# Attention sink as a 129th score column, the u product by halves of positions, and an even table of fillers

## The chip, the cores and the metric

The kernel runs on one core of a Trainium2 chip. The metric is the device time of one execution in microseconds (us), the median of several; smaller is better. The core has five engines with instruction queues of their own: TensorE (PE; its weight loads are counted apart as PEld), VectorE (DVE), ScalarE (ACT), GpSimd (POOL) and SyncE (SP), which here issues DMA transfers. Engines wait for each other through semaphores.

## The reference

One layer of a hybrid decoder trunk on 1024 positions of width 1024, in float32. Only the first third matters here:

```
h = rmsnorm(x)
[q | k | v | u | s | gate_a | gate_b] = h @ w_in
A: q, k by heads of 64, RMS norm; windowed attention in blocks of 128 queries against
   the 256 keys of the block before and of its own; scores minus slope * distance;
   softmax over these and one learned "sink" per head, whose weight is then dropped
B: u * (tril(W_s) @ rmsnorm(v) + b), in chunks of 128 positions
x = x + (sigmoid(gate_a) * (A @ w_oa) + sigmoid(gate_b) * (B @ w_ob)) @ w_out
x = x + down(silu(conv(up_g)) * conv(up_v))
```

There are 8 query heads, 2 key heads, and 8 blocks of 128 queries. The products want more than one pass at the fast matmul type, so an operand is split into a high part (`...h`) and a low part (`...l`, the operand minus the high part), and three products hh, hl and lh are summed (`mm3`).

## The kernel before, in words

The program starts with the products for k, v and the first q, then runs the attention loop, then the V phase (rmsnorm of v, the triangular products), the gates, the output product, and for most of the time the feed-forward part. The change lies in the attention loop and in two constants that it uses.

The loop has 20 steps. A unit of attention work, n = 0 to 15, is four heads of one block of queries (half n // 8, block n % 8), and it goes down a pipeline of several steps. All engines take their instructions in the order in which the loop is written. Step n issues on TensorE: the scores of unit n (`s_mm`, tile `sc`, eight matmuls of 128x256), the products with v of unit n-4 (`pv_mm`, tile `pv`), a first filler, the transposes of the probabilities of unit n-2 (`p_trans`, tile `pt`), a second filler, and the transposes of q for unit n+2 (`q_trans`, tile `pqt`). The two fillers are what the table FILL says for that step, one letter each: q is a q projection (`q_proj`, 24 matmuls of 128x256), u is one sixteenth of the u product (`u_chunk`, 12 matmuls of 128x512), v is half of the v product for one block of positions (`v_half`, 24 matmuls of 128x256, tile `pvs`).

What the other engines do for a unit, in the order of its steps:

- `s_mask`: VectorE picks the masked scores (copy_predicated; each query sees a window of 128 of the 256 keys, so the two halves of the keys fold into one tile of 128x4x128), and adds the distance penalty `ali`, which gives `c`.
- `s_max`: VectorE takes the row maximum, then the negated maximum against the negated sink (`nsink`), then the sink less the maximum. These go into the small tile `sm`.
- `s_exp`, one step later: ScalarE takes four exponentials (one for each head, with the row sum) and a small one of the sink, VectorE adds that to the sums and takes the reciprocal, GpSimd multiplies `c` by it.
- `p_split`: ScalarE copies the transposed tile to `ch`, VectorE makes `cl`, and GpSimd separates each into the keys of the block before (`eh`, `el`) and of the own block (`ch`, `cl`) by four affine_selects.
- `pv_out`: ScalarE and VectorE add the two halves of `pv` into `ya`, which SyncE stores after the last block of a half.

A u chunk covers two of the eight blocks of the contraction and all 1024 positions: four chunks make one tile `pu` of two PSUM banks, which VectorE then evacuates into uT in one instruction of 128x1024 (L679). `pu` and `sc` come from the same pool (`PS`, two buffers of two banks each) and take turns. `pt`, `pv`, `pq`, `pqt` and two of the `pvs` tiles come from another (`PH`, one bank each).

GpSimd's queue holds more than this: the low parts of weights that arrive during the loop (`weights(n)`: ScalarE makes the high part, GpSimd the low part; v0 at step 13, v1 at 14, z0 at 16, z1 at 17), and, towards the end, the triangular mask of s (L792) and its low part (L795). The load of s (L99) uses a raw buffer that v1's split sets free. After unit 15, input rows are loaded again (`rows_again(1)`, L617) into the buffer of `ya`.

Of the kernel before, what the change touches and what calls it, by code (L numbers as in the profile page):

```python
# [10 lines left out]
F = mybir.dt.float32  # L11
R = mybir.dt.float32r
U8 = mybir.dt.uint8
AF = mybir.ActivationFunctionType
# [9 lines left out]
NEG = -1e30  # L24
# [3 lines left out]

ROWS = (slice(0, 64), slice(64, 128))
X_AHEAD = 5  # L30
FILL = "qu|q|qu|qu|uu|q|qu|qu|q|qu|qu|qu|q|uu|u|u|uu|vv|v|v".split("|")
WHEN = {"u1": 0, "q0": 1, "q1": 2, "u2": 5, "u3": 9, "v0": 13, "v1": 14, "z0": 16, "z1": 17}


# [7 lines left out]
def body(ctx, tc, nc, a):  # L42
# [8 lines left out]
    def nm(s):  # L51
        uid[0] += 1
        return f"{s}_{uid[0]}"
# [37 lines left out]
    def mm3(out, wh, wl, mh, ml, first, last, **kw):  # L91

        nc.tensor.matmul(out, wh, mh, start=first, stop=False, **kw)  # L93
        nc.tensor.matmul(out, wh, ml, start=False, stop=False, **kw)  # L94
        nc.tensor.matmul(out, wl, mh, start=False, stop=last, **kw)  # L95
# [231 lines left out]
    nc.vector.tensor_scalar(kgq, cp[:, 184:185], cp[:, 185:186], 0.125, op0=ALU.mult, op1=ALU.mult)  # L327
# [118 lines left out]
    def s_mask(n):  # L446

        half, b = divmod(n, 8)
        p4 = st.pop(("ps", n))
        hs = slice(4 * half, 4 * half + 4)  # L450
        c = tm.tile([128, 4, 128], F, tag="c", name=nm("c"), bufs=3)
        if b == 0:
            nc.vector.tensor_tensor(c, p4[:, :, 0:128], ali[:, hs, :], op=ALU.add)
            nc.gpsimd.affine_select(out=c, in_=c, pattern=[[0, 4], [-1, 128]], compare_op=ALU.is_ge,
                                    fill=NEG, base=0, channel_multiplier=1)
        else:
            nc.vector.copy_predicated(p4[:, :, 128:256], msk, p4[:, :, 0:128])
            nc.vector.tensor_tensor(c, p4[:, :, 128:256], ali[:, hs, :], op=ALU.add)
        st[("c0", n)] = c

    def s_max(n):
        hs = slice(4 * (n // 8), 4 * (n // 8) + 4)
        c = st.pop(("c0", n))
        sm = tm.tile([128, 4, 4], F, tag="sm", name=nm("sm"), bufs=3)
        nc.vector.tensor_reduce(sm[:, 0, :], c, axis=AX.X, op=ALU.max)
        nc.vector.scalar_tensor_tensor(sm[:, 0, :], sm[:, 0, :], -1.0, nsink[:, hs], op0=ALU.mult, op1=ALU.min)
        nc.vector.tensor_tensor(sm[:, 2, :], sink_b[:, hs], sm[:, 0, :], op=ALU.add)
        st[("c", n)] = (c, sm)

    last_exp, last_sel = [None], [None]  # L470

    def s_exp(n):
        c, sm = st[("c", n)]
        m, den, es = sm[:, 0, :], sm[:, 1, :], sm[:, 2, :]
# [3 lines left out]
        nc.scalar.activation(es, es, AF.Exp)  # L478
        nc.vector.tensor_tensor(den, den, es, op=ALU.add)
        nc.vector.reciprocal(den, den)  # L480
        nc.gpsimd.tensor_tensor(c, c, den.unsqueeze(2).to_broadcast([128, 4, 128]), op=ALU.mult)

    def p_trans(n):
        c = st.pop(("c", n))[0]
        p = PH("pt")
        for i in range(4):
            nc.tensor.transpose(p[:, i * 128:(i + 1) * 128], c[:, i, :], ident)
        st[("pt", n)] = p.rearrange("p (h q) -> p h q", q=128)
# [58 lines left out]

    n_q, n_u, n_v, u_done = [4], [0], [0], []
    pvs = {}
# [9 lines left out]
    def filler(n, i):  # L559

        kind = FILL[n][i:i + 1]
        if kind == "q":
            q_proj(n_q[0])
            n_q[0] += 1
            return [n_q[0] - 1]
        if kind == "v":
            v_half(n_v[0], 0)
            n_v[0] += 1
        if kind == "u":
            t = u_chunk(n_u[0])  # L570
            n_u[0] += 1
            if t is not None:
                u_done.append((t, ust["p"]))
        return []

    wv = []
# [70 lines left out]
    for n in range(20):  # L647
# [27 lines left out]
            x_sums((0, 1), True)  # L675
        if n == 19:
            x_sums((2, 3), True)
        for t, p in u_done:
            nc.vector.tensor_tensor(uT[:, t, :], p, rstd_b, op=ALU.mult)  # L679
        u_done.clear()  # L680
        if n + 2 < 16:
            q_trans(n + 2)
# [1295 lines left out]
def layout(x, mix_norm, w_in, q_norm, k_norm, sinks, sgu_norm, w_s, b_s,  # L1978
# [35 lines left out]
    ali = -slopes[None, :, None] * dist[:, None, :]  # L2014
# [31 lines left out]
```

## Time and profile before

| | us |
| --- | --- |
| median of 3 runs (range) | 1183.58 (1183.52 to 1184.87) |
| span of the profiled execution | 1183.5 |
| TensorE busy in the span | 1170.3 |
| VectorE busy | 874.5 |
| GpSimd busy | 631.8 |
| ScalarE busy | 566.5 |
| attention loop from step 2 to its end | 59 to 180 |

A line of the profile gives the engine, the line of the kernel, the operation, output and input by their names in the program, and the shape. In a timeline the first two numbers are the start and the duration in us; a wait stands in brackets with what ended it. Groups have their count, busy time and mean in ns. The profiled execution's own time is its span but for what lies ahead of the first instruction and behind the last, and at 1183.5 it is at the median of the runs.

### The profile page before, as it was taken

What the parts mean: (1) busy time and instruction counts of PE and PEld (TensorE: products, weight loads), DVE (VectorE), ACT (ScalarE), POOL (GpSimd) and SP (SyncE); (2) the same over time, 40 slices, a digit from 0 to 9 for tenths busy, and PEclk for the clock granted to TensorE, in tenths of its full rate; (3) what the DMA queues carried; (4) which work ended last, traced back from release to release, by engine and by line L of the source; (5) the groups of instructions that cost most, each with busy time, mean ns of one, the idle gap of its engine ahead of it and who ended that gap; (6) DMA issues with size and microseconds to landing.
All of it is one profiled execution on the core that took longest, in us unless ns stands there. A gap on an engine that the chain in (4) does not pass through costs nothing.

```text
span 1183.5 us, 15928 instructions
## 1 busy us (share of the span) xinstructions
PE 1170.3 (99%) x5842; PEld 990.4 (84%) x5842; DVE 874.5 (74%) x1037; ACT 566.5 (48%) x878; POOL 631.8 (53%) x435
## 2 busy tenths in 40 slices
PE   8999999999999999999999999999999999999998
PEld 8989989988888878888878888888888888888887
DVE  7798975743536776678788788877888797875674
ACT  8555667644336653335444443444444445425331
POOL 2467685488884764444867677776767541000000
PEclk9999999999999999999999999999999999999999
DMA  7110136157556654454545445455555268975471
GB/s 272 37 55 19 54 130 228 56 168 239 161 160 204 233 193 154 146 176 132 138 129 169 118 149 152 142 141 134 166 137 160 72 219 287 365 232 196 155 231 67
DMA packets 80942, 188.66 MB, mean 159 GB/s; under 512 B 9184, under 2 KB 16864, under 8 KB 80736
## 3 DMA queue, kind: packets, MB, share of 16 engines
q1 hardware_dynamic: 73008, 167.58, 40.7%
q0 software_dynamic: 7456, 15.73, 8.0%
q10 hardware_dynamic: 400, 4.33, 1.1%
q8 instruction: 46, 0.75, 0.3%
q14 instruction: 32, 0.26, 0.1%
HBM read 146.97 MB, written 49.02 MB: 166 GB/s over the span
## 4 chain that ended last, share of the span: by engine, by line
PE 82%; DVE 4%; POOL 3%; ACT 2%; issue 2%; DMA 1%; DVEq 0%; POOLq 0%; SPq 0%; ACTq 0%
PE pz L1060 50%; PE pd L1855 10%; PE pdy L1855 8%; PE px L95 2%; PE px L93 2%; PE px L94 2%; PE pu L95 1%; PE pu L93 1%; PE pu L94 1%; PE pv L517 1%; PE pq L93 1%; PE pq L95 1%; PE pq L94 1%; DVE xa L621 1%; DMA lq<-wup 0%
## 5 line engine op out<-in xcount | busy, mean ns | idle before, releaser
L1060 PE MATMUL pz<-T,qh 128*128 128x512 f32 x472 | 145.6, 390 | 0.0
L1060 PE MATMUL pz<-B,ph 128*128 128x512 f32 x352 | 109.7, 393 | 0.7 <-ACT x L1695 0.7
L1060 PEld LDWEIGHTS pz<-T,qh 128*128 128x128 f32 x472 | 88.4, 188 | 18.6 <-ACT u L885 0.3
L1019 POOL TENSOR_TENSOR pl<-lp,ph 128x1024 fp32r<-128x1024 f32 x30 | 73.2, 2439 | 52.9 <-ACT ph L89 52.9
L1060 PE MATMUL pz<-T,ql 128*128 128x512 f32 x236 | 91.8, 389 | 0.0
L1019 POOL TENSOR_TENSOR ql<-lq,qh 128x1024 fp32r<-128x1024 f32 x30 | 76.8, 2559 | 9.1 <-ACT qh L89 9.1
L1060 PEld LDWEIGHTS pz<-B,ph 128*128 128x128 f32 x352 | 65.1, 188 | 16.7 <-ACT x L1695 3.8
L1078 DVE TENSOR_TENSOR pz<-pz,rstd_b 128x1024 f32<-128x1024 f32 x60 | 73.9, 1232 | 4.6 <-ACT rstd_b L143 2.5
L1060 PE MATMUL pz<-T,s3h 128*128 128x512 f32 x232 | 71.4, 389 | 0.0
L1060 PE MATMUL pz<-y,wjh 128*128 128x512 f32 x224 | 69.5, 391 | 0.6 <-POOL y L1233 0.3
L1060 PE MATMUL pz<-B,pl 128*128 128x512 f32 x176 | 68.6, 390 | 0.0
L1855 PE MATMUL pd<-bh,ah 128*128 128x512 f32 x176 | 68.5, 389 | 0.0
L1855 PE MATMUL pd<-bl,ah 128*128 128x512 f32 x176 | 68.5, 389 | 0.0
L1855 PE MATMUL pd<-bh,al 128*128 128x512 f32 x176 | 68.5, 389 | 0.0
L1060 PE MATMUL pz<-T,AX 128*128 128x512 f32 x264 | 63.4, 389 | 0.0
L1060 PE MATMUL pz<-B,AX 128*128 128x512 f32 x264 | 63.4, 389 | 0.0
L1019 POOL TENSOR_TENSOR s3l<-lq,s3h 128x512 fp32r<-128x512 f32 x20 | 26.0, 1298 | 62.3 <-ACT s3h L89 62.3
L1060 PEld LDWEIGHTS pz<-T,AX 128*128 128x128 f32 x264 | 49.5, 188 | 10.3
L1060 PEld LDWEIGHTS pz<-B,AX 128*128 128x128 f32 x264 | 49.6, 188 | 10.3
L89 ACT ACTIVATE AX<-lr 128x1024 fp32r<-128x1024 f32 x22 | 23.4, 1063 | 70.9 <-POOL lr L621 70.9
L621 DVE TENSOR_TENSOR pz<-pz,u 128x512 f32<-128x512 f32 x37 | 25.9, 700 | 42.5 <-ACT u L1072 36.2
L1550 DVE SCALAR_TENSOR_TENSOR tg<-pz,cp,tg 128x1023 f32<-128x1023 f32 (+1 forms) x44 | 56.2, 1278 | 0.8
(359 smaller groups left out, 3597.6 us busy)
## 6 DMA issues: line engine op xcount, KB each, us to landing
lp<-wup SPq DMA_DIRECT2D x22, 512.0 KB, 3.8
lq<-wup SPq DMA_DIRECT2D x22, 512.0 KB, 4.2
ra<-wdown SPq DMA_DIRECT2D x44, 256.0 KB, 4.9
b<-T SPq DMA_DIRECT2D x44, 256.0 KB, 3.5
lq<-wup POOLq DMA_DIRECT2D x42, 256.0 KB, 5.3
B<-tv SPq DMA_DIRECT2D x33, 256.0 KB, 2.0
T<-tt SPq DMA_DIRECT2D x33, 256.0 KB, 2.1
b<-B SPq DMA_DIRECT2D x33, 256.0 KB, 3.0
```

What stands on the lines that cost most here:

```text
L89: return nc.scalar.activation(dst, src, AF.Copy, scale=scale)
L93: nc.tensor.matmul(out, wh, mh, start=first, stop=False, **kw)
L94: nc.tensor.matmul(out, wh, ml, start=False, stop=False, **kw)
L95: nc.tensor.matmul(out, wl, mh, start=False, stop=last, **kw)
L517: nc.tensor.matmul(o, vhl[:, kb, g, :], w[:, 2 * g:2 * g + 2, :], start=i == 0 and g == 0, stop=i == len(ops) - 1, skip_group_check=True)
L621: eng.tensor_tensor(out, x, y, op=op)
L1019: nc.gpsimd.tensor_tensor(l, r, h.bitcast(F), op=ALU.subtract)
L1060: nc.tensor.matmul(o, p[:, k, :], m, start=not more and k == 0 and j == 0, stop=k == nk - 1 and j == 2, skip_group_check=True)
L1078: nc.vector.tensor_tensor(z, z, rstd_b, op=ALU.mult)
L1550: nc.vector.scalar_tensor_tensor(t[:, j:], p[:, 0:1024 - j], cw[:, ci, 2 - j:3 - j], t[:, j:], op0=ALU.mult, op1=ALU.add)
L1855: nc.tensor.matmul(o[d], p[:, k - k0, m], q[:, k - k0, :], start=new and k == 0 and j == 0, stop=k == HK - 1 and j == 2, skip_group_check= ...
```

## The change

Three edits in the attention loop.

The sink becomes a column of the tile. The tile is now 129 wide for each head: 128 columns hold the negated scores (kgq and ali have their signs turned), and the last the negated sink, which ScalarE copies in for each unit. One minimum over 129 columns is the negated maximum; the exponentials take scale -1 and sum over 129 columns. The two small VectorE instructions of `s_max`, the small exponential, and the addition of it to the sums are no more. GpSimd's multiplication works on 128 of each 129 columns.

The u product goes by halves of positions. A chunk covers four blocks of the contraction and 512 positions, one bank; two chunks make a half, which VectorE evacuates in one instruction of 128x512. One `pu` tile is taken from `PS` for all 16 chunks, and given back after the last.

FILL is another: one q and one u in each of steps 0 to 11, one u in steps 12 to 15, one v in 16 and 17, two in 18, none in 19.

```diff
-FILL = "qu|q|qu|qu|uu|q|qu|qu|q|qu|qu|qu|q|uu|u|u|uu|vv|v|v".split("|")
+FILL = "qu|qu|qu|qu|qu|qu|qu|qu|qu|qu|qu|qu|u|u|u|u|v|v|vv|".split("|")
...
-        c = tm.tile([128, 4, 128], F, tag="c", name=nm("c"), bufs=3)
+        cs = tm.tile([128, 4, 129], F, tag="c", name=nm("c"), bufs=3)
+        c = cs[:, :, 0:128]
+        nc.scalar.copy(cs[:, :, 128], nsink[:, hs])
...
-        nc.vector.tensor_reduce(sm[:, 0, :], c, axis=AX.X, op=ALU.max)
-        nc.vector.scalar_tensor_tensor(sm[:, 0, :], sm[:, 0, :], -1.0, nsink[:, hs], op0=ALU.mult, op1=ALU.min)
-        nc.vector.tensor_tensor(sm[:, 2, :], sink_b[:, hs], sm[:, 0, :], op=ALU.add)
-        st[("c", n)] = (c, sm)
+        nc.vector.tensor_reduce(sm[:, 0, :], cs, axis=AX.X, op=ALU.min)
+        st[("c", n)] = (cs, sm)
...
         for i in range(4):
-            last_exp[0] = nc.scalar.activation(c[:, i, :], c[:, i, :], AF.Exp, bias=m[:, i:i + 1],
+            last_exp[0] = nc.scalar.activation(cs[:, i, :], cs[:, i, :], AF.Exp, bias=m[:, i:i + 1], scale=-1.0,
                                                accum_out=den[:, i:i + 1])
-        nc.scalar.activation(es, es, AF.Exp)
-        nc.vector.tensor_tensor(den, den, es, op=ALU.add)
         nc.vector.reciprocal(den, den)
         nc.gpsimd.tensor_tensor(c, c, den.unsqueeze(2).to_broadcast([128, 4, 128]), op=ALU.mult)
...
     def u_chunk(i):
-        t, j = divmod(i, 4)
-        if j == 0:
+
+        t, h, j = i // 4, i // 2 % 2, i % 2
+        if i == 0:
             ust["p"] = PS("pu")
-        p, (wh, wl) = ust["p"], ust[("w", t)]
-        for k in (2 * j, 2 * j + 1):
-            for h in range(2):
-                c = slice(h * 512, (h + 1) * 512)
-                mm3(p[:, c], wh[:, k, :], wl[:, k, :], hx(0, k, c), hx(1, k, c), k == 0, k == 7)
-        return t if j == 3 else None
+        wh, wl = ust[("w", t)]
+        c = (L, H)[h]
+        p = ust["p"][:, c]
+        for k in range(4 * j, 4 * j + 4):
+            mm3(p, wh[:, k, :], wl[:, k, :], hx(0, k, c), hx(1, k, c), k == 0, k == 7)
+        return (t, c, p) if j else None
...
-        for t, p in u_done:
-            nc.vector.tensor_tensor(uT[:, t, :], p, rstd_b, op=ALU.mult)
+        for t, c, p in u_done:
+            nc.vector.tensor_tensor(uT[:, t, c], p, rstd_b[:, c], op=ALU.mult)
```

What stands in the queues at the places that the prediction uses (a name's number tells one tile from another; a lone "..." leaves rows out). First VectorE, one softmax step in the first half of the loop. Before:

```order
L457 COPY_PREDICATED sc_1024<-msk,sc_1024 128x4x128
L458 TENSOR_TENSOR c_1033<-sc_1024,ali 128x512
L479 TENSOR_TENSOR sm_952<-sm_952 128x4
L480 RECIPROCAL sm_952<-sm_952 128x4
L465 TENSOR_REDUCE sm_1044<-c_1033 128x4
L466 SCALAR_TENSOR_TENSOR sm_1044<-sm_1044,nsink 128x4
L467 TENSOR_TENSOR sm_1044<-sink_b,sm_1044 128x4
L530 TENSOR_TENSOR ya_682<-pv_1048,o_1083 64x2x128 x2
```

VectorE in the same step, now:

```order
L459 COPY_PREDICATED sc_1028<-msk,sc_1028 128x4x128
L460 TENSOR_TENSOR c_1037<-sc_1028,ali 128x4x128
L477 RECIPROCAL sm_957<-sm_957 128x4
L466 TENSOR_REDUCE sm_1047<-c_1037 128x4
L527 TENSOR_TENSOR ya_682<-pv_1049,o_1096 64x2x128 x2
```

Three rows are gone: the addition of the sink's exponential ahead of the reciprocal, and the two rows behind the reduction.

TensorE in the last steps before the V phase, from the last chunk of u on (`pv` of unit 13 begins with eh_2147; `pt_2257` is unit 15; each pvs row stands for 24 that differ in x and in the pass). Before:

```order
L517 MATMUL pv_2223<-eh_2147,vhl 128x256 x2
...
L517 MATMUL pv_2223<-cl_2144,vhl 128x256 x2
L93 MATMUL pvs_2232<-wv_2004,x_3_116 128x256
...
L487 MATMUL pt_2257<-ident,c_2097 128x128 x4
L93 MATMUL pvs_2262<-wv_2004,x_3_116 128x256
...
L517 MATMUL pv_2306<-eh_2213,vhl 128x256 x2
...
L93 MATMUL pvs_2315<-wv_2004,x_3_116 128x256
...
L517 MATMUL pv_2349<-eh_2296,vhl 128x256 x2
...
L93 MATMUL pvs_2358<-wv_2004,x_3_116 128x256
```

TensorE at the same place now (`pv` of unit 13 begins with eh_2126, `pt_2235` is unit 15):

```order
L93 MATMUL pvs_2153<-wv_1990,x_3_116 128x256
...
L484 MATMUL pt_2178<-ident,c_2013 128x128 x4
L514 MATMUL pv_2201<-eh_2126,vhl 128x256 x2
...
L93 MATMUL pvs_2210<-wv_1990,x_3_116 128x256
...
L484 MATMUL pt_2235<-ident,c_2079 128x128 x4
L514 MATMUL pv_2259<-eh_2192,vhl 128x256 x2
...
L93 MATMUL pvs_2268<-wv_1990,x_3_116 128x256
...
L93 MATMUL pvs_2293<-wv_1990,x_3_116 128x256
...
L514 MATMUL pv_2327<-eh_2249,vhl 128x256 x2
L93 MATMUL pvs_2153<-wvB_2198,x_3_116 128x256
```

The v halves have moved up: one stands ahead of pv of unit 13, one between units 13 and 14, and two between units 14 and 15, where it was two between 13 and 14, one between 14 and 15, and one behind the last. Nothing now stands between a `pt` and the `pv` that follows it, where a u chunk or a v half was.

More of the change, by code (lines that the diff above doesn't have):

```diff
@@ L326, in body @@
     nc.vector.tensor_scalar(nsink, sink_b, -1.0, None, op0=ALU.mult)
[L327 removed]
+    nc.vector.tensor_scalar(kgq, cp[:, 184:185], cp[:, 185:186], -0.125, op0=ALU.mult, op1=ALU.mult)
     nc.vector.tensor_copy(ss8, p_ssq[:, 0:16].rearrange("p (s two) -> p s two", two=2)[:, :, 0])
@@ L454, in s_mask @@
             nc.gpsimd.affine_select(out=c, in_=c, pattern=[[0, 4], [-1, 128]], compare_op=ALU.is_ge,
-                                    fill=NEG, base=0, channel_multiplier=1)
+                                    fill=-NEG, base=0, channel_multiplier=1)
         else:
@@ L458, in s_mask @@
             nc.vector.tensor_tensor(c, p4[:, :, 128:256], ali[:, hs, :], op=ALU.add)
-        st[("c0", n)] = c
+        st[("c0", n)] = cs
     def s_max(n):
-        hs = slice(4 * (n // 8), 4 * (n // 8) + 4)
-        c = st.pop(("c0", n))
-        sm = tm.tile([128, 4, 4], F, tag="sm", name=nm("sm"), bufs=3)
-        nc.vector.tensor_reduce(sm[:, 0, :], c, axis=AX.X, op=ALU.max)
-        nc.vector.scalar_tensor_tensor(sm[:, 0, :], sm[:, 0, :], -1.0, nsink[:, hs], op0=ALU.mult, op1=ALU.min)
-        nc.vector.tensor_tensor(sm[:, 2, :], sink_b[:, hs], sm[:, 0, :], op=ALU.add)
-        st[("c", n)] = (c, sm)
+        cs = st.pop(("c0", n))
+        sm = tm.tile([128, 2, 4], F, tag="sm", name=nm("sm"), bufs=3)
+        nc.vector.tensor_reduce(sm[:, 0, :], cs, axis=AX.X, op=ALU.min)
+        st[("c", n)] = (cs, sm)
     last_exp, last_sel = [None], [None]
     def s_exp(n):
-        c, sm = st[("c", n)]
-        m, den, es = sm[:, 0, :], sm[:, 1, :], sm[:, 2, :]
+        cs, sm = st[("c", n)]
+        m, den, c = sm[:, 0, :], sm[:, 1, :], cs[:, :, 0:128]
         for i in range(4):
-            last_exp[0] = nc.scalar.activation(c[:, i, :], c[:, i, :], AF.Exp, bias=m[:, i:i + 1],
+            last_exp[0] = nc.scalar.activation(cs[:, i, :], cs[:, i, :], AF.Exp, bias=m[:, i:i + 1], scale=-1.0,
                                                accum_out=den[:, i:i + 1])
-        nc.scalar.activation(es, es, AF.Exp)
-        nc.vector.tensor_tensor(den, den, es, op=ALU.add)
         nc.vector.reciprocal(den, den)
@@ L483, in p_trans @@
     def p_trans(n):
-        c = st.pop(("c", n))[0]
+        c = st.pop(("c", n))[0][:, :, 0:128]
         p = PH("pt")
@@ L569, in filler @@
         if kind == "u":
-            t = u_chunk(n_u[0])
+            u = u_chunk(n_u[0])
             n_u[0] += 1
-            if t is not None:
-                u_done.append((t, ust["p"]))
+            if u:
+                u_done.append(u)
+            if n_u[0] == 16:
+                del ust["p"]
         return []
@@ L2013, in layout @@
     slopes = np.array([2.0 ** -(h + 1) for h in SP], np.float32)
-    ali = -slopes[None, :, None] * dist[:, None, :]
+    ali = slopes[None, :, None] * dist[:, None, :]
     return {
```

## The prediction

> **What bounds the kernel now.** I read the page first (busy times, then the chain that ended last), then the busy times of the attention stage, then TensorE's waits there, then its timeline around each wait. The page:
>
> ```profile
> PE 1170.3 (99%) x5842; PEld 990.4 (84%) x5842; DVE 874.5 (74%) x1037; ACT 566.5 (48%) x878; POOL 631.8 (53%) x435
> PE 82%; DVE 4%; POOL 3%; ACT 2%; issue 2%; DMA 1%; DVEq 0%; POOLq 0%; SPq 0%; ACTq 0%
> ```
>
> TensorE is busy 99% of a 1183.5 us span, and 82% of the chain is TensorE. The change issues the same matmuls (the same number of q, u and v fillers, the same transposes), so it can gain only what TensorE now stands still in the attention loop, and lose only what new stalls it makes there or behind. The loop, from step 2 to the end, by window (busy time of each engine, granted clock, DMA share):
>
> ```profile
> 59.00:180.00 121.00, 117.90 (x826) 107.53 (x825) 103.97 (x218) 72.30 (x233) 86.56 (x95) 1.00 0.19 66
> ```
>
> VectorE is at 86% and GpSimd at 72%: neither is the bound, but each is near enough that its queue can be late. The granted clock is 1.00 here, so no time is in the throttle. TensorE's waits in this window (total us, times, longest):
>
> ```profile
> PE pv L517 <- POOL cl L505: 1.0, 2, 0.5
> PE sc L439 <- DVE c L458: 0.6, 1, 0.6
> PE pv L517 <- DVE ya L530: 0.6, 2, 0.4
> PE sc L439 <- DVE uT L679: 0.4, 1, 0.4
> PE pq L93 <- DVE cl L496: 0.3, 2, 0.2
> ```
>
> Eight waits, 2.9 us. A wait in this view is shorter than what it costs, since a matmul's modelled end overlaps its successor. The true loss is start to start against the same pair without a wait:
>
> ```profile
> 82.26 0.38 PE L295 MATMUL pqt<-ident,qr 128*128 128x128 f32 x2
> 83.05 0.35 PE L439 MATMUL sc<-kT,qs 128*128 128x256 f32 x1 [0.41 <-DVE uT L679]
> 118.91 0.38 PE L295 MATMUL pqt<-ident,qr 128*128 128x128 f32 x2
> 119.05 0.48 PE L439 MATMUL sc<-kT,qs 128*128 128x256 f32 x2
> 127.05 0.36 PE L439 MATMUL sc<-kT,qs 128*128 128x256 f32 x1
> ```
>
> (The last row is the next step's sc: a step without a stall lasts 8.0 us.) The second pair takes 0.14 us, the first 0.79: 0.65 lost where 0.41 is shown, so 0.24 more for each wait. That makes 2.9 + 8 x 0.24 = 4.8. Two pairs stretch by 0.28 and 0.25 with no wait shown (a pt transpose at 162.76, an el pass at 177.98), together 0.5. With slow restarts (the first matmul after a wait is 0.1 longer in some rows) **all of TensorE's stalls in the loop are worth 5.3 to 5.6 us, and I take 5.5**; this is the ceiling of the direct gain.
>
> Six of the ten stalls lie before 160 us and are VectorE's: c, uT, ya or cl came late. By the same count they are worth 1.9 + 6 x 0.24 = 3.3, with restarts some 3.5. The other four, in the tail, are GpSimd's or follow on these:
>
> ```profile
> 163.18 0.48 PE L93 MATMUL pu<-x,wuh 128*128 128x512 f32 x1
> 165.99 0.40 PE L517 MATMUL pv<-eh,vhl 128*128 128x256 f32 x2
> 167.27 0.50 PE L517 MATMUL pv<-cl,vhl 128*128 128x256 f32 x2 [0.41 <-POOL cl L505]
> 167.60 0.28 PE L93 MATMUL pvs<-wv,x 128*128 128x256 f32 x1
> 170.33 0.60 PE L487 MATMUL pt<-ident,c 128*128 128x128 f32 x4
> 177.98 0.50 PE L517 MATMUL pv<-el,vhl 128*128 128x256 f32 x2
> 179.02 0.51 PE L517 MATMUL pv<-cl,vhl 128*128 128x256 f32 x2 [0.54 <-POOL cl L505]
> ```
>
> These rows also give the fillers: a u chunk 165.99 - 163.18 = 2.81 (about 2.77 without its slow first matmul), a v half 170.33 - 167.60 = 2.73.
>
> **The change part by part.**
>
> The softmax on VectorE loses three small instructions a step (x15 or 16), whose mean times are far above what 16 values for each partition need:
>
> ```profile
> 159.53 2.20 DVE L466 SCALAR_TENSOR_TENSOR sm<-sm,nsink 128x4 f32<-128x4 f32 x1
> L466 DVE SCALAR_TENSOR_TENSOR sm<-sm,nsink 128x4 f32<-128x4 f32 x15 | 10.3, 688 | 0.5
> L467 DVE TENSOR_TENSOR sm<-sink_b,sm 128x4 f32<-128x4 f32 x15 | 4.0, 268 | 0.5
> L479 DVE TENSOR_TENSOR sm<-sm 128x4 f32<-128x4 f32 x16 | 9.1, 568 | 0.0
> L478 ACT ACTIVATE sm<-sm 128x4 f32<-128x4 f32 x15 | 2.8, 189 | 0.0
> ```
>
> 10.3 + 4.0 + 9.1 = 23.4 us of VectorE's 104 go, 1.5 a step. The 2.20 us case stands beside a GpSimd split that runs from 159.27 (its row follows below). TensorE's only gain from this is the VectorE stalls, at most 3.5. The reduction and the exponentials are 129 wide in place of 128: under 1% of instructions of 0.66 and 0.41, nothing. ScalarE loses the fourth kind of row above (0.19 a step) and gains a copy of 128x4 that nothing of this trace equals but the row of 0.19: even. It is queued ahead of the previous step's exponentials and reads a constant; what it waits for is that its c buffer be free (three in turn, the same count as now), long before. Signs (scale -1, minimum, -0.125) cost nothing.
>
> The u product goes by halves of positions. Every chunk is still 12 matmuls of 128x512 in the same form, now all on one bank: the v halves above run 24 in a row on one bank at 0.114 for 256 columns, just half of the 0.23 for 512, so 0. The evacuation becomes 8 of 128x512 in place of 4 of 128x1024:
>
> ```profile
> L679 DVE TENSOR_TENSOR uT<-pu,rstd_b 128x1024 f32<-128x1024 f32 x4 | 4.9, 1215 | 0.0
> L496 DVE TENSOR_TENSOR cl<-pt,ch 128x512 fp32r<-128x512 f32 x16 | 11.1, 691 | 4.2 <-POOL c L481 3.0 <-ACT ch L89 0.8
> ```
>
> 8 x 0.69 - 4 x 1.22 = 0.6 us more on VectorE, against 23.4 less. The pu tile takes its two banks once for the loop; the score tiles then turn over without it, and the wait of sc on uT (0.65) has no ground left. In turn, chunk 2i+4 writes the bank that was evacuated two chunks earlier: a step of 8 us and more of cover, so 0.
>
> The filler table puts one q and one u into each of steps 0 to 11, then u to step 15, v at 16 and 17, vv at 18. Steps become even, and by the middle of the loop no VectorE stall should be left. But u is done earlier, so the tail has less TensorE work between one transposed probability tile and its use. GpSimd's queue has the same order as now. It must be walked. Before, pt of block 11, ScalarE's copy of it, GpSimd's rows that matter and the load of s stand here:
>
> ```profile
> 145.26 0.60 PE L487 MATMUL pt<-ident,c 128*128 128x128 f32 x4
> 145.95 0.60 ACT L89 ACTIVATE ch<-pt 128x512 fp32r<-128x512 f32 x1 [2.26 <-PE pt L487]
> 159.27 2.44 POOL L193 TENSOR_TENSOR wv<-v,wv 128x1024 fp32r<-128x1024 f32 x1
> 161.68 1.03 POOL L481 TENSOR_TENSOR c<-c,sm 128x512 f32<-128x512 f32 x1
> 161.74 0.33 SPq L99 DMA_DIRECT2D s<-ws  x1
> 165.53 1.09 POOL L792 TENSOR_SCALAR_AFFINE_SELECT s<-s 128x1024 f32<-128x1024 f32 x1
> 166.58 0.64 POOL L505 TENSOR_SCALAR_AFFINE_SELECT cl<-cl 128x512 fp32r<-128x512 f32 x1
> 168.18 2.42 POOL L795 TENSOR_TENSOR wgl<-s,wgh 128x1024 fp32r<-128x1024 f32 x1
> 170.54 0.65 POOL L503 TENSOR_SCALAR_AFFINE_SELECT eh<-ch 128x512 fp32r<-128x512 f32 x1
> 172.56 0.64 POOL L505 TENSOR_SCALAR_AFFINE_SELECT cl<-cl 128x512 fp32r<-128x512 f32 x1
> ```
>
> Step by step. (a) Until pt(11) the new table runs three more u chunks than the old (14 against 11), and about 3.5 us of stalls go: 145.26 - 3.5 + 3 x 2.77 = 150.1. (b) From its selects, 1.3 us later (145.95 + 0.60 - 145.26), GpSimd should be back to back: selects(11) 2.6, v0's split 2.4, c 1.0, selects(12) 2.6, v1's split 2.4, from 151.4 to 162.4. Before, v1's split ended at 161.71: GpSimd is 0.7 late. The select of a block is 172.56 + 0.60 - 170.54 = 2.6. (c) The load of s goes out when v1's raw buffer is free, and its select came 165.53 - 161.74 = 3.8 later: 166.1 to 166.2, 0.5 or 0.6 later than now. The rest of the chain is the same work in the same order, so cl(13) ends at 167.7 and cl(14) at 173.7 (before 167.2 and 173.16). (d) TensorE after pt(11): 20.7 us lay between pt(11) and pv(13) before, 0.4 of it stall, with five u chunks; now two and one v half, 5.6 less: pv(13) starts at 150.1 + 14.8 = 164.9 to 165.0, needs cl(13) 0.7 later and gets it at 167.7. **It loses 2.05.** (e) Then a v half and pt(15), pv(14) starts at 171.3, needs cl(14) at 172.0, gets it at 173.7: **it loses 1.75.** (f) Behind it lie two v halves, 5.5 us, in which selects(15) finish; pv(15) doesn't wait.
>
> Each has a slow restart, 0.05 here. **Sum: 5.5 - 2.05 - 1.75 - 0.1 = 1.6.** Behind cl(14) GpSimd has z0's split, selects(15) and z1's split, 2.4 + 2.6 to 3.4 + 2.4: it ends at 181.1 to 181.9. The V phase begins near 180.5 with the half that z0 feeds, and comes to z1's 1.4 us later at the earliest, so this can cost 0.1 and no more. The profiled execution's span is 1183.5, the median 1183.58, the same within 0.1. **Forecast: 1183.6 - 1.6 = 1182.0.**
>
> One price has no row: GpSimd's multiplication by 1/den now reads and writes four rows of 128 with a gap of one value between them. Lower bound 0: row 161.68 already takes a broadcast operand in four pieces and lasts 1.03. The nearest row above it on the same size is
>
> ```profile
> 190.93 1.29 POOL L621 TENSOR_TENSOR lq<-lq 128x512 f32<-128x512 f32 x1
> ```
>
> which bounds it at 0.26 more; a gain isn't to be had from a gap. Three multiplications lie in the GpSimd chain that sets (d) and (e), so 0 to +0.8. I take 0, since the row of 1.03 has the same operation and broadcast, and keep 0.8 for the range.
>
> [...]
>
> **The rivals.**
>
> A, no late GpSimd (chance 0.22). If (b) isn't back to back, say since the even steps let v0's and v1's splits begin earlier, cl(13) and cl(14) are in time. Then all 5.5 go: 1178.1, and half of it 1180. For it: GpSimd idles 28% of the window. Against it: a split waits for the selects ahead of it in the queue, and these for pt(11), which by (a) is 4.8 later.
>
> B, the gain is given back later (0.10). The second set of input rows is loaded into the buffer of ya, after its store:
>
> ```profile
> 181.28 0.80 SPq L533 DMA_DIRECT2D ya<-ya  x2
> 185.61 2.15 SPq L617 DMA_DIRECT2D xa<-xw  x4
> ```
>
> That store follows pv(15), and pv(15) comes only 1.6 earlier; but if selects(15) or the output sums are later than I have them, the load, ScalarE's gain on it and then the V phase's products slip against a TensorE that is ahead. The loss is at most the gain: 1183.0 to 1183.6.
>
> C, slower (0.07). The gapped multiplication is dear. Every tenth of a microsecond on it delays cl(13) and cl(14) by 0.2 to 0.3. To end over 0.2% (2.4 us) behind, the three would have to cost 1.6 + 2.4 = 4.0, 1.3 each, 1.04 to 2.34: then 1186. For it: the row has no like. Against it: nothing of 128x512 on GpSimd is over 1.3 in these rows.
>
> D, the change doesn't do what it says (0.03): if the one pu tile were tracked as a whole, each half's first chunk would wait for the other half's evacuation. In steps of 8 us with a chunk of 2.8 that is 5 us before the chunk is due, price 0; in the short steps from 12 on it could cost the old 0.65 once or twice: 1182.0 to 1183.3.
>
> **How the numbers follow.** The forecast has 0.58, with its own range 1181.2 to 1182.9 (stride bound upward, VectorE stalls and (b) downward by 0.8). The range goes down to 1179.5, so that it holds the nearer half of A, and up to 1184.5 for B and the cheap end of C; some 2 in 10 remain outside. A measurement of this kernel tells about 0.2%, 2.4 us, from no change: below 1181.2 is faster. Faster: A and a little of the forecast, 0.28. Slower, above 1185.9: C and a remnant, 0.08. Same: 0.64.
>
> **What would show it.** Right: no wait of sc on uT or c and none of pq on cl between 60 and 160; pv on GpSimd's cl twice in the tail, at about 1.9 and 1.6 in the waits; VectorE's busy time in the loop about 23 us less; pt(11) near 150.1; the multiplication near 1.04. Wrong: waits of pv on cl that are absent (A), or longer than 3 us each with a multiplication over 2 (C), or a V phase that starts near 180.5 and then waits on the reloaded rows (B). If uT or ya still hold TensorE in the middle, the 3.5 was put down wrongly to what is removed.

## The result, and the profile after

| | before | after |
| --- | --- | --- |
| median of 9 runs each (range), us | 1183.97 (1183.52 to 1184.87) | 1186.59 (1185.27 to 1188.18) |
| ratio after to before, 95% interval | | 1.0020 (1.0011 to 1.0029) |
| span of the profiled execution, us | 1183.5 | 1185.5 |

The change makes the kernel 0.2% slower, some 2.4 us, where 1.6 us of gain were forecast. The runs after spread over 2.9 us, those before over 1.35. One execution among the experiments, the profiled one of e1, ran at a mean granted clock of 0.655 and took 1677.61 us; ratios leave it out. The time of a run is 1.7 to 1.8 us above its span (1187.21 against 1185.5 in the profiled execution of after), so the profiled execution of before stood for about 1185.2, 1.2 above its median, and not at the median as the prediction had it. The two profiles are compared with each other.

The page of after, the same two parts as before:

```profile
PE 1169.8 (99%) x5842; PEld 990.3 (84%) x5842; DVE 852.7 (72%) x993; ACT 566.5 (48%) x878; POOL 631.0 (53%) x435
PE 88%; DVE 3%; DMA 3%; POOL 3%; ACT 2%; issue 2%; SPq 0%; DVEq 0%; POOLq 0%; ACTq 0%
```

VectorE has 21.8 us less to do. TensorE's busy time is within 0.5 us of what it was, and the chain holds 3% of DMA where it held 1%. The attention loop's window and all of TensorE's waits in it (after):

```profile
59.00:180.00 121.00, 118.44 (x838) 108.77 (x837) 82.74 (x175) 72.02 (x230) 85.79 (x95) 1.00 0.19 66
PE pv L514 <- POOL cl L502: 1.9, 2, 1.7
PE pv L514 <- POOL eh L500: 0.3, 1, 0.3
PE pv L514 <- POOL ch L502: 0.2, 1, 0.2
```

The waits on c, ya, uT and VectorE's cl are gone, and those on GpSimd have grown. TensorE's timeline of after at the places of the prediction's walk, and further:

```profile
149.78 0.60 PE L484 MATMUL pt<-ident,c 128*128 128x128 f32 x4
164.91 0.48 PE L514 MATMUL pv<-eh,vhl 128*128 128x256 f32 x2
167.60 0.50 PE L514 MATMUL pv<-cl,vhl 128*128 128x256 f32 x2 [1.74 <-POOL cl L502]
173.55 0.50 PE L514 MATMUL pv<-cl,vhl 128*128 128x256 f32 x2 [0.20 <-POOL cl L502]
180.24 0.39 PE L514 MATMUL pv<-cl,vhl 128*128 128x256 f32 x2
180.47 0.28 PE L93 MATMUL pvs<-wvB,x 128*128 128x256 f32 x1
...
198.93 0.38 PE L93 MATMUL pvs<-wv,x 128*128 128x256 f32 x1 [1.34 <-DVE vg L760]
...
220.36 0.39 PE L93 MATMUL pm<-wgh,vsh 128*128 128x256 f32 x1 [1.53 <-ACT pm L926]
```

The row at 180.24 is the last product of unit 15. Before, it stood at 179.02. And the last two kinds of row before:

```profile
182.10 0.28 PE L93 MATMUL pvs<-wvB,x 128*128 128x256 f32 x1
...
218.26 0.39 PE L93 MATMUL pm<-wgh,vsh 128*128 128x256 f32 x1 [0.52 <-ACT pm L926]
```

At the start of the V phase (the first product with wvB) the changed kernel is 182.10 - 180.47 = 1.63 us ahead, as forecast. At the pm product it is 220.36 - 218.26 = 2.10 behind, and so it ends. **The V phase gave back 3.7 us.** About 0.5 of this is no wait: the first 120 products of the V phase come every 0.118 us, where they came every 0.113 before, and the cause of that isn't shown. What released the rest stands in the chain of after, in order of time:

```profile
182.38 0.33 SPq L530
182.75 3.94 DMA ya<-ya
186.75 0.33 SPq L617
187.13 7.64 DMA xa<-xw
194.80 1.15 ACT xa L631
```

The last store of ya, then the load of input rows into ya's buffer, then ScalarE's gain on them. The store went out at 181.28 before, and at 182.38 now. ScalarE's rows, before and then after:

```profile
191.11 2.18 ACT L631 ACTIVATE xa<-xa,cp 128x1024 f32<-128x1024 f32 x2
```

```profile
192.38 1.15 ACT L631 ACTIVATE xa<-xa,cp 128x1024 f32<-128x1024 f32 x1 [2.71 <-DMA xa<-xw]
194.80 1.15 ACT L631 ACTIVATE xa<-xa,cp 128x1024 f32<-128x1024 f32 x1 [1.26 <-DMA xa<-xw]
```

Before, the rows were there when ScalarE came to them. Now it waits 2.71 and 1.26 us in the middle of its queue, and the gelu of the next block of v, on which vg and then TensorE's pvs buffers depend, stands behind. The store is only a part of it. The load of the first row, before and then after, with the time from issue to landing at the end:

```profile
xa<-xw SPq DMA_DIRECT2D x1, 512.0 KB, 3.6
```

```profile
xa<-xw SPq DMA_DIRECT2D x1, 512.0 KB, 5.5
```

Before, it went out at 185.61 and landed 1.9 us ahead of ScalarE. Now it goes out 1.1 later and takes 1.9 longer, and ScalarE is there 1.4 earlier (free at 189.67): 1.1 + 1.9 + 1.4 - 1.9 = 2.5 of the 2.7. Why the load takes longer isn't shown.

### The profile page after: what moved, and what is told of

Same layout as the page of the kernel before. It is cut to its first block, busy times and chain, and to the rows that moved or that the text cites. A ratio compares the mean times of both kernels' runs of the same rounds, so it can differ in the third digit from the quotient of the medians.

```text
span 1185.5 us, 15852 instructions
## 1 busy us (share of the span) xinstructions
PE 1169.8 (99%) x5842; PEld 990.3 (84%) x5842; DVE 852.7 (72%) x993; ACT 566.5 (48%) x878; POOL 631.0 (53%) x435
## 4 chain that ended last, share of the span: by engine, by line
PE 88%; DVE 3%; DMA 3%; POOL 3%; ACT 2%; issue 2%; SPq 0%; DVEq 0%; POOLq 0%; ACTq 0%
PE pz L1060 50%; PE pd L1855 10%; PE pdy L1855 8%; PE px L95 2%; PE px L93 2%; PE px L94 2%; PE pu L93 1%; PE pu L95 1%; PE pu L94 1%; PE pq L93 1%; PE pq L95 1%; PE pq L94 1%; PE pv L514 1%; PE pkv L95 1%; PE pkv L93 1%
## 5 line engine op out<-in xcount | busy, mean ns | idle before, releaser
L1550 DVE SCALAR_TENSOR_TENSOR tv<-pz,cp,tv 128x1023 f32<-128x1023 f32 (+1 forms) x44 | 56.3, 1278 | 0.8
```

Of the source, the lines that this page charges most:

```text
L1550: nc.vector.scalar_tensor_tensor(t[:, j:], p[:, 0:1024 - j], cw[:, ci, 2 - j:3 - j], t[:, j:], op0=ALU.mult, op1=ALU.add)
```

## The experiments

Sums of stalls below are taken from the traces as in the prediction: start to start of consecutive matmuls, less the median spacing of that shape in the trace of before, where more than 0.04 us is left. By that count the profile of before has 5.4 us of stalls from 59 to 160, 2.4 from 160 to 180 and 0.8 from 180 to 240; after has 2.4, 4.0 and 3.8. Each kernel's ratio is to the kernel before, run beside it on the same chip (medians of before beside them: 1184.3 to 1184.6). Behind 225 us, where no edit changes anything, the same instructions take up to 1.3 us more or less in one profile than in that of before; the cause is open, so differences of that size between two kernels aren't explained here.

### The late reload

**e1_rows_early**, the changed kernel with:

```diff
+    def rows_into_ya(ks):
+        for k in ks:
+            nc.sync.dma_start(ya[:, k, :], a["xw"][4 + k, :, 257:1281])
...
         if n == 15:
             rows_again(0)
+            rows_into_ya((0, 1))
...
-    rows_again(1)
+    rows_into_ya((2, 3))
+    xr_raw.append(ya)
```

> The changed kernel, but the second set of input rows goes into the tile of ya itself, two of its four rows right after the first set (their part of ya was stored half a loop earlier) and only the other two behind the last store. Reload theory: the loss behind 180.5 us comes from pv of the last unit standing behind two v halves, so that the store of ya, the reload and ScalarE's gain on it (queued ahead of the gelu) come late; with two rows early ScalarE waits 0 in place of 2.7 and 1.3 us, TensorE's wait of pvs on vg (1.3 shown) goes, and the time falls by 3 to 4 us to 1182.5 to 1183.5. Rival (order theory): the V phase is bound by ScalarE's and VectorE's queues whenever TensorE arrives early; then the time falls by less than 1 us and stays at 1185.7 to 1186.6.

Measured: 1182.64, ratio 0.9982 (0.9973 to 0.9991). From 0.2% slower to 0.2% faster by moving two loads. Its profile is that of a second run of the same kernel, **e9_rows_early_again**:

> The same kernel as the one with the early rows (the changed kernel, two of four input rows loaded early into ya's tile), run once more for a profile at full clock. Reload theory: no wait of ScalarE on the rows, no wait of pvs on vg, the V phase begins at 180.5 as in the changed kernel and the pm product near 216.7 in place of 220.4; the two waits of pv on GpSimd's cl (about 1.9 and 1.4 from start to start) stay. One time near 1182.6.

1182.94 in one run. ScalarE's rows and TensorE's waits from 59 to 225 (two views of e9):

```profile
189.90 2.18 ACT L635 ACTIVATE ya<-ya,cp 128x1024 f32<-128x1024 f32 x2
196.16 1.15 ACT L635 ACTIVATE ya<-ya,cp 128x1024 f32<-128x1024 f32 x1 [0.22 <-DMA ya<-xw]
```

```profile
PE pv L514 <- POOL cl L502: 1.9, 1, 1.9
PE pm L93 <- ACT pm L932: 0.5, 1, 0.5
```

The waits on rows fall to 0.2, pvs no longer waits on vg, and pm is back at 0.5. The spacing of 0.118 us is gone too, so up to 0.5 us of what is won need not be the reload's. The reload theory holds, and the order theory (less than 1 us) falls.

**e2_before_rows_early**: the same edit in the kernel before.

> The kernel before with the same early reload and nothing else. Reload theory: ScalarE did not wait for the rows there (its gain began at 191.11 right behind the work ahead of it), so the time stays within 0.5 us of before, 1183.5 to 1184.5. Rival (the reload bound the kernel before too): 1.5 us or more faster.

1184.89, ratio 0.9999 (0.9990 to 1.0008). The reload was covered there: the edit is worth nothing by itself.

**e4_before_two_v**: the kernel before with the end of the change's table.

```diff
-...|uu|u|u|uu|vv|v|v
+...|uu|u|u|uu|vv|vv|
```

> The kernel before with one edit, the end of the table uu|vv|vv| in place of uu|vv|v|v: pv of the last unit behind two v halves. Reload theory: TensorE loses its last wait on cl (0.5 shown, 1.1 with the stretch around it) and starts the V phase 1.1 us earlier, near 181.0, but the store of ya comes 1 to 1.5 us later, and the kernel becomes slower by 1.5 to 2.5 us, 1185.5 to 1186.5, with waits of ScalarE on the rows. Order theory: it becomes faster by up to 1.1, 1183.

1189.69, ratio 1.0038 (1.0026 to 1.0051), 5 us slower, more than twice the expected loss. The V phase does start earlier (180.63), but then (TensorE's waits, 180 to 225):

```profile
PE pvs L93 <- DVE vg L760: 2.1, 1, 2.1
PE pz L1060 <- DVE vg L760: 1.6, 1, 1.6
PE pm L93 <- ACT pm L926: 1.5, 1, 1.5
```

Two of these are the waits of after. The pz wait (pz is the first product behind the V phase) stands in neither kernel. Here pz starts at 223.97, when the last vg row is done (223.91); before and after, it starts ahead of that row (219.75 against 220.73, 221.89 against 222.83). One reading is that pz takes over PSUM banks of pvs tiles, and that the last blocks of v lie in other banks, since one v half and the last pv have changed places. No run tests it. **e8_before_two_v_rows_early** adds the early rows:

> The kernel before with the table's end uu|vv|vv| (which cost 5 us by itself) and, beside it, two of the second set of input rows loaded early into ya's tile. Reload theory: the loss of 5 us goes, since its cause was ScalarE waiting for these rows ahead of the gelu; what is left is TensorE's last wait that the table removes, so 0.5 to 1.2 us faster than before, 1183.2 to 1184.2. Order theory (the V phase suffers whenever TensorE arrives early, or the v halves of that order are bad in themselves): at least 3 us slower than before stay.

1185.66, ratio 1.0011 (1.0002 to 1.0020): 4 of the 5 us go, some 2 less than the reload theory expected, and the 3 us that the order theory wanted to see stay don't. The pz wait of 1.6 stays and takes back what the V phase had won: it begins 1.8 earlier than before (180.34 against 182.10), and at pz the two are level (219.78 against 219.75). The 1.1 us by which this profile is longer than that of before come behind pz, with no cause shown. So the order theory isn't wholly wrong: with that order of v halves there is a wait of its own in this kernel.

**e3_tail_one_v**: the changed kernel with one v half in each of the last steps.

```diff
-...|u|u|u|u|v|v|vv|
+...|u|u|u|u|v|v|v|v
```

> The changed kernel with the end of the table u|u|u|u|v|v|v|v: one v half stands ahead of pv of the last unit in place of two, and the fourth behind it. Reload theory: pv of the last unit then waits about 2.5 us for GpSimd's cl (ready near 179.2), the V phase begins 1.2 to 1.5 us later, near 181.9, but the store of ya and the reload come about 1.1 us earlier, as in the kernel before; the time falls by 1.5 to 3 us, to 1183.7 to 1185. Order theory: TensorE's later start is what counts, the time rises by 1 to 1.5 us, to about 1187.8.

1188.36, ratio 1.0026 (1.0014 to 1.0037): far from the reload theory's time and near the order theory's 1187.8. But the run doesn't separate them, since the store moved by 0.5 us only, to 181.89, and the V phase began at 180.74, not near 181.9. VectorE's rows say why the store is late:

```profile
177.38 3.61 DVE L621 TENSOR_TENSOR xa<-xa 128x512 f32<-128x512 f32 x2
181.00 0.86 DVE L527 TENSOR_TENSOR ya<-pv,o 64x256 f32<-64x256 f32 x2
```

pv of the last unit was done at 178, but ya stood in VectorE's queue behind two sums on the first input rows, which took 1.8 us each beside GpSimd's split of z1. ScalarE then waits for rows as in after (2.46 and 2.44), and pz waits 1.6 as in e4. Stall from 180 to 240: 7.1, of which some 1.7 belongs to the granted clock (last section).

### The parts of the change

**e6_sink_alone**: of the change's diff only `s_mask`, `s_max`, `s_exp`, `p_trans` and the signs of kgq and ali; in short, against the kernel before:

```diff
+        cs = tm.tile([128, 4, 129], F, tag="c", name=nm("c"), bufs=3)
...
+        nc.vector.tensor_reduce(sm[:, 0, :], cs, axis=AX.X, op=ALU.min)
...
-        nc.vector.tensor_tensor(den, den, es, op=ALU.add)
```

> The kernel before with the sink column alone; table and u chunks as before. By the prediction's step on VectorE: the waits of TensorE on c, ya and cl between 60 and 160 go (2.4 us of start-to-start loss), the wait of sc on uT (0.65) stays, and VectorE's busy time in the loop falls by some 23 us. In the tail, GpSimd then is late by up to 1.5. Time 0.5 to 2 us faster than before, 1182.5 to 1184. Rival (those waits came from the table, not from the small instructions): the waits between 60 and 160 stay at 1.9 us and the time within 0.5 us of before.

1179.22, ratio 0.9958 (0.9944 to 0.9972): **5 us faster**, three more than the range expected at its best. All that is left of waits from 59 to 180, and what GpSimd waited for there, before and then in e6:

```profile
PE sc L439 <- DVE sm L477: 0.6, 1, 0.6
```

```profile
POOL c L481 <- DVE sm L480: 9.9, 12, 2.7
POOL ch L505 <- DVE cl L496: 4.2, 3, 1.6
POOL ch L505 <- DVE sm L479: 1.1, 1, 1.1
```

```profile
POOL c L478 <- DVE sm L477: 14.4, 7, 4.4
POOL ch L502 <- DVE cl L493: 0.2, 1, 0.2
```

GpSimd's queue in the tail was waiting for VectorE in the middle of a unit's four selects: 1.64 us at 149.40, 1.64 at 157.38, 1.05 at 164.35 in the trace of before. With 48 small instructions gone from VectorE these waits go (what is left, ahead of the multiplication, is idle time of a GpSimd that is early), and with them TensorE's waits on GpSimd's cl: 0.2 us of stall from 160 to 180 where before had 2.4, and a V phase that starts at 177.07 in place of 182.10. The wait of sc on uT goes too, with the old u chunks.

**e7_fill_and_u_alone**: table and u halves, with the softmax of before; against the kernel before:

```diff
-FILL = "qu|q|qu|qu|uu|q|qu|qu|q|qu|qu|qu|q|uu|u|u|uu|vv|v|v".split("|")
+FILL = "qu|qu|qu|qu|qu|qu|qu|qu|qu|qu|qu|qu|u|u|u|u|v|v|vv|".split("|")
...
+        p = ust["p"][:, c]
```

> The changed table and the u product by halves, with the softmax of the kernel before. By the prediction's step: the wait of sc on uT goes and some VectorE waits stay (0.5 to 1.5 us between 60 and 160); the tail and the reload are as in the changed kernel. Time between the changed kernel's and 2 us above it, 1186.5 to 1188.5. Rival (the table alone removes all waits in the middle): the same as the changed kernel within 0.5 us.

1189.38, ratio 1.0043 (1.0030 to 1.0055): 5 us slower, just above the range expected. From 59 to 180:

```profile
PE pv L517 <- POOL cl L505: 1.5, 3, 1.1
PE pv L517 <- POOL ch L505: 1.1, 2, 0.9
PE pu L93 <- DVE uT L682: 0.9, 1, 0.9
PE pvs L94 <- POOL wv L193: 0.4, 1, 0.4
PE pv L517 <- POOL eh L503: 0.3, 1, 0.3
```

So the two parts don't simply add up: the sink column is worth 5.0 us with the old table and u chunks, and 2.7 with the new (ratios 1.0043 and 1.0020). The start of the V phase shows the same, 5.0 earlier by it there (182.10 to 177.07) and 2.8 here (183.31 to 180.47). With the new table TensorE still waits for GpSimd in the tail when VectorE is no longer late, as the waits of after show.

**e10_old_table**: sink column and u halves with the old table; against the changed kernel:

```diff
-FILL = "qu|qu|qu|qu|qu|qu|qu|qu|qu|qu|qu|qu|u|u|u|u|v|v|vv|".split("|")
+FILL = "qu|q|qu|qu|uu|q|qu|qu|q|qu|qu|qu|q|uu|u|u|uu|vv|v|v".split("|")
```

> The changed kernel with the table of the kernel before; sink column and u by halves stay. If the u halves cost and bring nothing, as the prediction had it, the time is that of the sink column alone, 1178.7 to 1179.8, and the new table alone accounts for the 7 us to the changed kernel. Rival (the halves carry part of the loss, by VectorE's eight evacuations or by a bank that is freed late): 1 us or more above the sink column alone.

1181.34, ratio 0.9972 (0.9961 to 0.9983), 2 us above the sink column alone, as the rival had it; the two intervals just touch. The V phase starts 1.4 later than there (178.45 against 177.07), by one wait. TensorE's row and VectorE's evacuations before it:

```profile
158.08 0.50 PE L93 MATMUL pu<-x,wuh 128*128 128x512 f32 x1 [1.20 <-DVE uT L679]
```

```profile
145.60 0.69 DVE L679 TENSOR_TENSOR uT<-pu,rstd_b 128x512 f32<-128x512 f32 x1 [1.40 <-PE pu L95]
157.34 0.68 DVE L679 TENSOR_TENSOR uT<-pu,rstd_b 128x512 f32<-128x512 f32 x1
```

The chunk at 158.08 writes the bank that was evacuated at 145.60, and waits for the evacuation of the other, at 157.34. **e14_old_table_evac_first** tests that:

```diff
+        for t, c, p in u_done:
+            nc.vector.tensor_tensor(uT[:, t, c], p, rstd_b[:, c], op=ALU.mult)
+        u_done.clear()
         if 0 <= n - 4 < 16:
             pv_out(n - 4)
```

> The changed kernel with the old table (1181.3, with a wait of pu on VectorE's uT of 1.37 us in step 14), and the evacuation of a finished u half moved from the end of the step to ahead of ya. If the next chunk waits for the evacuation that has just been queued, that of the other bank, since the one pu tile is tracked as a whole, the wait goes or falls under 0.3, and the time to 1179 to 1180. If it waits for its own bank's evacuation, done two chunks earlier, nothing changes: 1181 to 1181.6.

The pu wait is gone, as it must be if the evacuation just queued was what it waited for. But the time is 1185.61, ratio 1.0010 (1.0001 to 1.0019), 4 us worse than e10. One VectorE row and two of TensorE's waits:

```profile
135.13 0.69 DVE L662 TENSOR_TENSOR uT<-pu,rstd_b 128x512 f32<-128x512 f32 x1 [3.65 <-PE pu L95]
```

```profile
PE pq L93 <- DVE cl L493: 1.4, 4, 0.7
PE pv L514 <- DVE ya L527: 1.0, 2, 0.5
```

At its new place the evacuation itself waits for the end of the chunk, and ya and cl, which were ready, stand behind it.

### GpSimd in the short steps

**e5_rows_early_dve_splits**: e1 with the four splits of v0, v1, z0 and z1 on VectorE (in `rsplit`).

```diff
-        nc.gpsimd.tensor_tensor(w[:, 1, ks, :], rv, w[:, 0, ks, :].bitcast(F), op=ALU.subtract)
+        eng.tensor_tensor(w[:, 1, ks, :], rv, w[:, 0, ks, :].bitcast(F), op=ALU.subtract)
...
-                rsplit(wv[0], raws[x], int(x[1]))
+                rsplit(wv[0], raws[x], int(x[1]), nc.vector)
...
-                rsplit(wv[1], raws[x], int(x[1]))
+                rsplit(wv[1], raws[x], int(x[1]), nc.vector)
```

> The changed kernel with the two early rows, and the low parts of v0, v1, z0 and z1 made by VectorE (which has room now) in place of GpSimd. GpSimd's queue in the tail loses 4 x 2.4 us, so the two waits of pv on cl (1.9 and 1.4 start to start) shrink to 0 to 1 in all, and TensorE begins the V phase 2.5 to 3.5 us earlier than at 180.47, near 177.5. If nothing is late behind it: 2.5 to 3.5 us faster than with the early rows alone, 1179 to 1180.5. Rival (the V phase's VectorE chain on the input rows gives it back): within 1 us of the early rows alone, 1181.7 to 1183.

1189.02, ratio 1.0033 (1.0020 to 1.0045); the profiled execution took 1185.5. Neither theory had it, and the V phase starts at 183.28, 2.8 later than in after. VectorE's split of v0 (1.66 at 153.06) stands ahead of uT, and the single pu tile makes TensorE wait for it:

```profile
155.37 0.50 PE L93 MATMUL pu<-x,wuh 128*128 128x512 f32 x1 [1.89 <-DVE uT L684]
```

Nor do pv's waits on GpSimd shrink: they lose 1.3 at 173.68 and 1.2 at 176.55 from start to start. Beside VectorE's splits GpSimd's selects last up to 1.62 us (at 172.00) where they take 0.64 otherwise, and one of the splits takes 3.46 (at 169.67) where that of v0 took 1.66. Why the other executions took 3 us more than the profiled one isn't settled; their mean granted clock was 0.994 to 0.995 against its 0.997.

**e12_splits_early** and **e11_splits_and_rows_early**: the splits stay on GpSimd, three steps earlier, without and with the early rows.

```diff
-"u3": 9, "v0": 13, "v1": 14, "z0": 16, "z1": 17
+"u3": 9, "v0": 10, "v1": 11, "z0": 13, "z1": 14
```

> The changed kernel with the low parts of v0, v1, z0 and z1 made at steps 10, 11, 13 and 14 in place of 13, 14, 16 and 17 (the new table uses up the weights whose place they take earlier). GpSimd theory: its tail is no longer late, the waits of pv on cl (1.9 and 1.4) go, and pv of the last unit, the store of ya and the V phase all begin about 3.5 us earlier; but the store stays late against TensorE, so the waits of ScalarE on the rows and of pvs on vg stay: 1182.5 to 1184. Rival (the splits are not what delays cl): the waits of pv on cl stay above 2 us in all and the time within 1 us of the changed kernel.

> The changed kernel with both: the four splits three steps earlier, and two input rows early. If the new table's whole damage is GpSimd's lateness in the tail and the late reload, no stall of note is left and the time comes to that of the sink column alone, 1178.5 to 1180. If something else of the table costs time, it stays at 1181 or above.

e12 1186.75, ratio 1.0019 (1.0011 to 1.0028), like after; e11 1182.51, ratio 0.9983 (0.9975 to 0.9992), like e1. Neither brought the gain expected of it. ScalarE's wait for the rows stays in e12, as expected (4.50). The large waits on cl are gone, but smaller ones of pv and pt took their place: 3.8 us of stalls from 160 to 180 in e11, 4.0 in after. GpSimd's row shows one reason: with v1 done, the mask of s was queued early and held the selects of a unit while the load was under way.

```profile
147.71 1.09 POOL L798 TENSOR_SCALAR_AFFINE_SELECT s<-s 128x1024 f32<-128x1024 f32 x1 [2.66 <-DMA s<-ws]
```

**e13_v_splits_in_long_steps**: the early rows, and against the changed kernel:

```diff
-"u3": 9, "v0": 13, "v1": 14, "z0": 16, "z1": 17
+"u3": 9, "v0": 6, "v1": 7, "z0": 12, "z1": 13
```

> The changed kernel with the two early rows, and the splits of v0 and v1 at steps 6 and 7 (long steps of 8 us), of z0 and z1 at 12 and 13. The mask of s and its low part follow early too, so GpSimd has some 7 to 8 us less to do in the short steps from 12 on. If GpSimd's amount of work in the short steps is what made pv wait, most of the 3 to 4 us of stalls between 150 and 180 goes: 1179 to 1180.5. If it is the length of the way from pt over ch and the selects to pv, which this does not shorten, pv goes on waiting in every short step: 1182 to 1183.

1179.15, ratio 0.9958 (0.9944 to 0.9971). No wait of TensorE is left from 59 to 180, 0.3 us of stalls from 160 to 180, and the V phase starts here:

```profile
176.78 0.28 PE L93 MATMUL pvs<-wvB,x 128*128 128x256 f32 x1
```

So it was what GpSimd has to do in the short steps, and not the length of the way from pt to pv, which this leaves as it was. The mask of s and its wait for the load went with the work, and e13 doesn't tell the two apart. A step with one u chunk is some 5.3 us of TensorE (pv of two units at 145.84 and 151.15 in e11), while selects 2.6, multiplication 1.0 and a split 2.4 are 6.0 of GpSimd; several such steps in a row add up. With both causes mended the new table is as good as the old one with the sink column alone (1179.15 and 1179.22), and these two are the fastest kernels of the study. The second needs the smaller edit.

## Why the prediction was wrong, point by point

**Right: the walk to the V phase.** pt(11) at 149.78 (150.1 forecast), pv(13) at 164.91 (164.9 to 165.0), a loss of 1.90 on its cl (2.05), cl(14) used at 173.55 (ready at 173.7), 1.4 lost there in four pieces (1.75), the V phase at 180.47 (180.5). That the gain at this place is 1.63 against 1.6 is in part luck: the losses are 0.5 smaller than forecast, and the slow restarts behind them cost 0.5 in place of 0.1. The waits that were to vanish before 160 did. VectorE lost 21.2 us in the window (23).

**The step that failed: "pv(15) comes only 1.6 earlier".** In rival B it was taken that pv of the last unit moves with the V phase. It doesn't: in the changed table both last v halves stand ahead of it, where one stood, so its last product comes at 180.24 in place of 179.02 and ya was stored at 182.38 in place of 181.28, 1.1 us later, while TensorE was 1.6 earlier. The table rows that tell this were in the part on the change, and the walk's own step (f) has the two halves there. With it, the load that was covered (e2: worth nothing) came 2.71 us late for ScalarE. Of that, 1.9 is the load's own length, 5.5 in place of 3.6, for which the prediction has no term.

**With it the bound of rival B, "at most the gain".** A chain released later than before has no reason to stop at the old time. The V phase lost 3.7 us: more than twice the gain of 1.6, against a price of 0 in the sum. e1 and e9 show that the reload is what this hung on, but for the 0.5 us of wider spacing. B was given 0.10.

**Put down to the wrong owner: the ceiling.** 5.3 to 5.6 us of stalls was right (the sink column alone brings 5.0), but not who owned them. The prediction gave VectorE 3.5 and put the tail's rest to GpSimd's own work. e6 shows that GpSimd was late there because it waited for VectorE; rows for this, GpSimd's waits on cl and sm, stood in the trace of before and were not used. The loss in the tail of after is then the table's: it puts GpSimd's splits beside short steps, and where they are moved away (e13) the V phase starts 3.7 earlier than in after.

**Rival C**, a dear multiplication on gapped rows, is out: the group of 16 has a mean of 1041 ns in both kernels. The 0.26 us that the prediction's row of 1.29 left open for each multiplication didn't come.

**Rival D**, one pu tile tracked as a whole, was given 0.03 and "price 0". It is what happens: e10's row and e14. In the changed kernel it costs 0.2 us, at 152.5, with the old table 1.4.

## What to carry to other kernels

Follow a change that pulls TensorE ahead until the next place where all engines meet, and list there each chain that doesn't start with TensorE's work: a store, a load into a buffer that the store frees, an in-order engine that will stand still on that load (here ScalarE, 2.71 and 1.26 us). When work is moved between steps of a loop, compare in each step what the slowest helper has to do with what TensorE has; evening out TensorE alone can make the helper the bound where its work isn't even (here 6.0 us of GpSimd in a step of 5.3). Test the parts of a change one by one: here one part was worth all of the gain, and the rest of the change took back more than that.

## What the runs showed of the hardware that was not expected

Very small VectorE instructions were not small: 128x4 at 688 ns on average in the loop with a case of 2.20 us beside a GpSimd split. (They hold four values for each partition, not 16 as the prediction says.) Removing three for each unit took some 22 us from the engine (874.5 to 852.7 in after), and 5 from the kernel (e6). Between 59 and 180 the trace of before has 46 such rows (L466, L467, L479). 17 have no GpSimd instruction beside them and take 0.15 to 0.17. 28 begin while one runs, take 0.27 to 2.20, and end 0.01 to 0.03 us behind it. The one left, at 158.56, lies beside the final 0.04 us of a select and takes 0.15. The row at 159.53 is one of the 28: it ends at 161.73, and the split that began at 159.27 ends at 161.71. The reciprocal of the same shape takes 0.18 all 16 times, also at 158.75, where a select runs beside it. What holds the other rows up isn't shown.

Behind five waits of TensorE of 2.06 to 2.99 us some 1.7 us more were lost each time. The window view of e3, behind its wait of 2.07 us that ended at 166.7 and the one of 2.99 that ended at 200.0 (both from start to start, less the usual spacing; the view shows start, length, the engines' busy times, then the granted clock):

```profile
167.40:170.80 3.40, 3.40 (x18) 3.40 (x17) 1.54 (x3) 1.95 (x4) 3.33 (x4) 0.50 0.54 220
201.50:204.90 3.40, 3.40 (x19) 3.40 (x18) 2.70 (x5) 3.31 (x7) 1.27 (x3) 0.50 0.47 154
```

For 3.4 us the granted clock was 0.50, and 128x256 matmuls came every 0.21 us in place of 0.11, about 1.7 us lost. The profiles have seven waits of 2.0 us or more in the loop and the V phase; five were followed by such a stretch (two in e3, one each in e7, e9 and e12), two weren't (e4, e5), and no other of these profiles has one there. What sets the clock down isn't shown. This loss may be a part of the wider spread of after's runs; that isn't shown, and it can't be all of it, since the longest run of after, 1188.18, had a mean granted clock of 0.999.
